# Accumulating DMAs for the residual rows of paired tiles, and a new order of loads in the second value block

## The chip, the cores and the metric

The kernel runs on one core of one Trainium2 chip. The metric is the device time of one execution in microseconds (us). Engine names as in the profile: PE is TensorE, DVE is VectorE, ACT is ScalarE, POOL is GpSimd, SP is the engine that only issues DMAs.

## The reference, cut to what matters

One layer of an encoder trunk on x of shape (2048, 1024), float32: a normalised input is projected to q, k, v and a gate, a 2-D neighbourhood attention mixes the tokens, the gated result is projected back, x is added, and a final normalisation follows.

```python
h = rmsnorm(x, g)
o, gate = neighbourhood_mixer(h, w_in, rpb)
x = x + (o * jax.nn.silu(gate)) @ w_out
return rmsnorm(x, norm_f)
```

The change touches two places: the projection to v (`h @ w_in`, columns of v), and the last line but one, where the residual x is added to the output projection.

## The kernel before, in words

All products are float32 done as three matmuls of split operands: a tile t is split into a high part (ACT copies it, rounding) and a low part (DVE subtracts the high part from t). A 128x512 result in PSUM takes 12 or 24 such matmuls.

The program is one long Python list of instructions. Every engine takes its own instructions in the order in which the Python wrote them, and each one waits for the tiles that it reads and for the buffers that it writes. Tiles come from pools with a fixed number of buffers in rotation (`raw` 6, `kp` 2, `ep` 2, `ev` 8, `rbp` 3, `qp` 2, `xp` 8, `wp` 8); a load into a pool waits until the tile that had the buffer has been read for the last time. SP issues nearly all DMAs, in order, so a load that waits for a buffer holds up every DMA behind it. Some steps are put off: `store(key, lag, f)` (L328) puts `f` into a list that `due(1)`, called after each matmul, works off when `lag` more matmuls have been written.

*Stage two* (`stage_two`, L801) makes q, k, v and the gate for the second half of the tokens. It begins with v: `pair(u, ts, *do)` (L834) writes the matmuls for the 128-token tiles `ts` and the weight block `u` (0 or 1) in four steps, and after step b calls `do[b]`, which holds the side work: `v` evacuates finished tiles, `lw(u, b)` loads two weight tiles into `raw`, `w(u, b)` splits them (L542 on ACT, L545 on DVE), `block`, `t123`, `form` prepare operands for the products that follow. Between them the rows of the output weights are prepared for later: `out_rows(k)` (L886) loads four tiles into `kp` and `ep`, `o(k, "+1")` is a sum on DVE (`out_sum`, L897) and `o(k, "=1")` a split (`out_split`, L904) whose parts SP stores to DRAM. There are four rounds, k = 0 to 3, all in the same four buffers. Then `run()` of `seven_products` starts (L438), whose first operands `ahead(-5)` forms (L420, L421).

*The paired rows.* Tiles 0 to 5 of the output are made singly (`outputs`, L1334). Tiles 6 to 15 go in five pairs, (6,7), (8,9), (10,11), (12,13), (15,14), each with seven products P instead of eight (`rows_product`, L1439), every product 12 matmuls (L1451), in three PSUM banks: P = 1 and 2 in one, 6, 7 and 4 in another, 5 and 3 in the third. A product may write on into its bank only when what must be read in between has been read. For a pair (n0, n1):

- P=1: ACT copies the bank to U1 (L1456). P=2: y of n0, left half (`add_rows`, L1248).
- P=6: DVE writes U6 = bank + U1 (L1461); GpSimd adds the residual x of n0, right half (L1464). P=7: U7 likewise, with x of n1, right half; then GpSimd adds x of n1, left half, to U1 itself (L1468).
- P=5: y of n1, right half = bank + U7. P=4: y of n1, left half = bank + U1, then `finish(n1)`. P=3: y of n0, right half = bank + U6, then `finish(n0)`.

The x tiles come by SP from DRAM (`load_rest_of`, L1434) into `rbp` and `qp`. After each y, ACT squares it and sums the squares (L1251, put off by 5 matmuls). `finish` puts off the root (DVE L1270, ACT L1271, DVE L1272, L1274), the scaling (L1291, two per tile) and the stores (L1295). Tile 14, the last but one, has its y multiplied by the final weights at once (L1256) and its scaling right behind the root (L1287, L1288); tile 15's right half is the last thing evacuated (L1234).

`rows_by_seven` (L1479) writes the order by hand: the first three pairs (E = 3) are interleaved, the last two go one after the other in the order 1, 6, 2, 7, 5, 4, 3. Loads of operands (L1420), their sums (`sum_rows`, L1432), loads of x and the forming of operands (`form_rows`, L1425 on ACT and L1426 on DVE, LEAD products ahead) are written after fixed products of that list.

Of the kernel before, what the change touches and what calls it, by code (L numbers as in the profile page):

```python
# [32 lines left out]
PLAIN = 6  # L33
# [38 lines left out]
def build(ctx, tc, x, xr, xt, wg, rpb, last, w_out, n0, nf, masks, out):  # L72
# [728 lines left out]
    def stage_two():  # L801
# [32 lines left out]
        def pair(u, ts, *do):  # L834
            for b in range(4):
                values_of(X2, u, ts, (2 * b, 2 * b + 1))
                if b < len(do):
                    do[b]()

        def both(*fs):  # L840
            return lambda: [f() for f in fs]
# [10 lines left out]
        def w(u, b):  # L852
            return lambda: [split_v(u, a, b) for a in range(2)]

        def lw(u, *bs):
            return lambda: [load_v0(u, a, b) for b in bs for a in range(2)]

        def v(u, *ts):
            return lambda: [evac_v(u, t, ps[t]) for t in ts]
# [26 lines left out]
        def out_rows(k):  # L886
            def g():
                for q, (r_, c_) in quarters.items():
                    OW[q] = kp([128, 960], F32, "ow")[:, :512] if r_ else ep([128, 512], F32, "ow")
                    nc.sync.dma_start(OW[q], w_out[(4 * r_ + k) * 128:(4 * r_ + k + 1) * 128, c_ * 512:c_ * 512 + 512])  # L890
            return g
# [24 lines left out]
        def o(k, *fs):  # L916
# [4 lines left out]
        pair(0, (10, 11), both(v(0, 8, 9), block("B22", x22, 2, 3)), t123(0), t123(1), both(lw(1, 1), *o(0, "+1")))  # L921
        pair(0, (12, 13), both(v(0, 10, 11), *o(0, "=1", "+3")), both(t123(2), *o(0, "=3", "+2")), both(t123(3), *o(0, "=2", "+4")),
             both(t4(0, 1, 2, 3), lw(1, 2), *o(0, "=4")))
        pair(0, (14, 15), both(v(0, 12, 13), w(1, 0), out_rows(1)), both(w(1, 1), lw(1, 3)), w(1, 2), w(1, 3))
        pair(1, (12,), v(0, 14, 15), both(form("T2", x11, 0), *o(1, "+1")), both(form("T2", x11, 1), *o(1, "=1")), both(*o(1, "+3")))
        pair(1, (13,), both(v(1, 12), form("T2", x11, 2), *o(1, "=3")), both(form("T2", x11, 3), *o(1, "+2")), both(*o(1, "=2", "+4")),
             both(*o(1, "=4")))
        pair(1, (14,), both(v(1, 13), form("T3", x22, 0), out_rows(2)), form("T3", x22, 1), both(), both(*o(2, "+1")))
# [295 lines left out]
    def add_rows(n, j, ps):  # L1224
        xr = RES.pop((n, j))
        state["event"] = clock[0]
        if n not in Y:
            Y[n] = [None, None], tiny.tile([128, 8], F32, name="st3")
        y, st = (raw if j and n < 3 else ev)([128, 512], F32, "y"), Y[n][1]
        Y[n][0][j] = y  # L1230
        if n == tiles - 1:
            cut = [slice(0, 256), slice(256, 512)] if j else [slice(0, 512)]
            for s in cut:
                nc.vector.tensor_tensor(y[:, s], ps[:, s], xr[:, s], OP.add)  # L1234
            for k, s in enumerate(cut):
                to = st[:, (j if k == 0 else 5):(j if k == 0 else 5) + 1]
                nc.scalar.activation(xr[:, s], y[:, s], AF.Square, scale=0.5 ** 0.5, accum_out=to)
            if j == 0:
                nc.vector.tensor_scalar(st[:, 6:7], st[:, 0:1], 0.5 * D * EPS, None, op0=OP.add)
                nc.scalar.activation(st[:, 7:8], st[:, 6:7], AF.Sqrt)  # L1240
            else:
                nc.vector.tensor_scalar(st[:, 7:8], st[:, 1:2], st[:, 6:7], None, op0=OP.add)
            w = ev([128, 512], F32, "yw")
            nc.vector.scalar_tensor_tensor(w, y, 0.5 ** 0.5 / NF_SCALE, late["nf"][j], op0=OP.mult, op1=OP.mult)
            Y[n][0][j] = w
            squared[0] += 1
            return
        nc.vector.tensor_tensor(y, ps, xr, OP.add)  # L1248

        def square():  # L1250
            nc.scalar.activation(xr, y, AF.Square, scale=0.5 ** 0.5, accum_out=st[:, j:j + 1])  # L1251
            squared[0] += 1

        if n == tiles - 2:
            w = ev([128, 512], F32, "yw")
            nc.vector.scalar_tensor_tensor(w, y, 0.5 ** 0.5 / NF_SCALE, late["nf"][j], op0=OP.mult, op1=OP.mult)  # L1256
            Y[n][0][j] = w
        store(("y", n, j), 5, square)

    def finish(n):  # L1260
        y, st = Y[n]
# [172 lines left out]
    def load_rest_of(m, j, k):  # L1434
        n = PAIRS[m][j]
        RES[n, k] = (qp if (j, k) == (1, 0) else rbp)([128, 512], F32, "xr")
        nc.sync.dma_start(RES[n, k], x[n * 128:n * 128 + 128, 512 * k:512 * k + 512])

    def rows_product(m, P):  # L1439
        n0, n1 = PAIRS[m]  # L1440
        if P in (1, 6, 5):
            B[m, P] = bank(512, "py")
            for Q in {1: (2,), 6: (7, 4), 5: (3,)}[P]:
                B[m, Q] = B[m, P]
        t = F.pop((m, P))
        f = uses[P][1]
        for k in range(4):
            c = slice(k * 128, k * 128 + 128)
            xh, xl = TF[f][k]
            for i, (a, b) in enumerate(((0, xh), (0, xl), (1, xh))):  # L1450
                nc.tensor.matmul(B[m, P], t[:, a, c], b, start=P in (1, 6, 5) and k == 0 and i == 0, stop=k == 3 and i == 2,  # L1451
                                 skip_group_check=True)
                due(1)
        if P == 1:
            U[m, 1] = (xp if m == 2 else ep)([128, 512], F32, "p1")
            nc.scalar.activation(U[m, 1], B[m, 1], AF.Copy)  # L1456
        elif P == 2:
            add_rows(n0, 0, B[m, 2])
        elif P in (6, 7):
            U[m, P] = xp([128, 512], F32, "u")  # L1460
            nc.vector.tensor_tensor(U[m, P], B[m, P], U[m, 1], OP.add)  # L1461
            to = (n0, 1) if P == 6 else (n1, 1)
            r = RES.pop(to)
            nc.gpsimd.tensor_tensor(U[m, P], U[m, P], r, OP.add)  # L1464
            RES[to] = U[m, P]
            if P == 7:
                r = RES.pop((n1, 0))
                nc.gpsimd.tensor_tensor(U[m, 1], U[m, 1], r, OP.add)  # L1468
                RES[n1, 0] = U[m, 1]
        elif P == 5:  # L1470
            add_rows(n1, 1, B[m, 5])
        elif P == 4:
            add_rows(n1, 0, B[m, 4])
            finish(n1)
        else:
            add_rows(n0, 1, B[m, 3])
            finish(n0)

    def rows_by_seven():  # L1479
        for f, (r, c) in plain_of.items():  # L1480
            TF[f] = [(woh[4 * r + k, c], wol[4 * r + k, c]) for k in range(4)]
        E, LEAD = 3, 4
        seq = [(m, P) for P in (1, 2) for m in range(E)]
        seq += [(0, 6), (1, 6), (0, 7), (0, 5), (1, 7), (0, 4), (1, 5), (0, 3), (1, 4), (2, 6), (1, 3), (2, 7), (2, 5), (2, 4), (2, 3)]
        seq += [(m, P) for m in range(E, len(PAIRS)) for P in order7]
# [10 lines left out]
            on(i, sum_rows, 2, f)  # L1496
        for i, f in ((2, "A21"), (4, "A22")):
            on(i, load_rows_of, 2, f)
        for i, m, j, k in ((1, 0, 1, 0), (2, 1, 1, 0), (4, 0, 0, 1), (5, 0, 1, 1), (6, 1, 0, 1), (7, 1, 1, 1), (9, 2, 0, 1), (9, 2, 1, 0),
                           (11, 2, 1, 1)):  # L1500
            on(i, load_rest_of, m, j, k)
        for m in range(E, len(PAIRS)):
            s = seq.index((m, 1))
            for d, f in ((-9, "A21"), (-8, "A22"), (-7, "A11"), (-6, "A12")):
                on(s + d, load_rows_of, m, f)
            for d, f in ((-5, "S1"), (-4, "S2"), (-3, "S3"), (-1, "S4")):
                on(s + d, sum_rows, m, f)
            for d, j, k in ((-2, 0, 1), (-2, 0, 0), (-1, 1, 0), (0, 1, 1)):
                on(s + d, load_rest_of, m, j, k)
        for i, s in enumerate(seq):  # L1510
            if i >= 2 * E:
                on(i - LEAD, form_rows, *s)
# [206 lines left out]
```

## Time and profile before

| | us |
|---|---|
| median of 3 runs | 1056.8 |
| the three runs | 1056.8, 1057.53, 1055.7 |
| the profiled execution | 1056.66 |
| its span, first to last instruction | 1054.9 |
| DVE busy in the span | 743.2 |
| ACT busy in the span | 558.4 |
| POOL busy in the span | 278.1 |
| bytes moved | 205.30 MB |

Rows of the timeline are: start in us from the span's start, duration in us, engine, line of the kernel, operation, output and inputs, and in brackets how long the engine had been idle before and what ended that. A row with xN joins N neighbours. "PEld" is the load of a matmul's weights and runs beside PE. "SPq" is an issue on SP's queue, not the transfer. A PE row's end is modelled: a matmul's row is 0.39 us long, while the next one starts sooner.

### The profile page before, as it was taken

To read this page: it belongs to the slowest core of one execution; us is meant where nothing else is said; L and a number is where in the kernel's file an instruction comes from. 1 tells how busy PE (TensorE), PEld (TensorE's weight loads), DVE (VectorE), ACT (ScalarE), POOL (GpSimd) and SP (SyncE) were. 2 spreads that over 40 slices of the span, in tenths; PEclk is the share of its full clock that TensorE was granted. 3 is DMA by queue.
4 is the path that set the end of the run, shared out by engine and by line. 5 is a ranking of instruction groups with operands and counts; after the bars stand their busy time and mean duration, and the time that the engine had idled before them with its cause. 6 is when DMAs were issued, how large, how long until landed. Compare 5 with 4: busy or idle time off the path is not lost.

```text
span 1054.9 us, 20328 instructions
## 1 busy us (share of the span) xinstructions
PE 1039.0 (98%) x7256; PEld 850.1 (81%) x7256; DVE 743.2 (70%) x1601; ACT 558.4 (53%) x1305; POOL 278.1 (26%) x357
## 2 busy tenths in 40 slices
PE   9999999999999989999999999999999999999987
PEld 6888888887888868888888788888888787888776
DVE  5385657778897847655565666667777788777996
ACT  7545323344344435333333477788887877673433
POOL 0000231321221000000000477765565432420331
PEclk9999999999999999999999999999999999999999
DMA  9633444452637568434243787868877689899442
GB/s 312 226 100 100 140 145 129 134 151 96 195 119 211 168 230 293 126 108 132 80 145 121 237 246 218 260 199 279 249 237 247 186 269 312 277 352 354 148 172 80
DMA packets 133213, 205.30 MB, mean 195 GB/s; under 512 B 12216, under 2 KB 56504, under 8 KB 133112
## 3 DMA queue, kind: packets, MB, share of 16 engines
q1 hardware_dynamic: 132680, 203.61, 60.7%
q8 instruction: 57, 0.93, 0.4%
q10 hardware_dynamic: 432, 0.40, 0.1%
q14 instruction: 44, 0.36, 0.1%
HBM read 145.24 MB, written 58.72 MB: 193 GB/s over the span
## 4 chain that ended last, share of the span: by engine, by line
PE 89%; DVE 7%; issue 1%; ACT 1%; DMA 1%; POOL 0%; ACTq 0%; DVEq 0%
PE pp L438 36%; PE pv L562 12%; PE s L1063 8%; PE o L1170 8%; PE py L1451 7%; PE ph L1148 4%; PE pp L384 2%; PE po L1372 2%; PE po L1374 2%; PE pp L386 2%; PE pp L382 2%; PE po L1376 2%; DMA raw<-in_wg_dram 1%; DVE l L521 1%; DVE y L1291 1%
## 5 line engine op out<-in xcount | busy, mean ns | idle before, releaser
L438 PE MATMUL pp<-h,f 128*128 128x512 f32 x672 | 217.6, 389 | 0.0
L1077 ACT ACTIVATE x<-x,st 128x360 f32<-128x360 f32 (+5 forms) x256 | 151.2, 592 | 24.6 <-DVE st L1071 24.6
L438 PEld LDWEIGHTS pp<-h,f 128*128 128x128 f32 x672 | 126.1, 188 | 26.5 <-DVE f L421 0.3
L438 PE MATMUL pp<-t,f 128*128 128x512 f32 x558 | 141.7, 389 | 0.1
L1091 POOL TENSOR_SCALAR x<-x,st 128x480 f32<-128x480 f32 (+5 forms) x192 | 114.4, 613 | 94.1 <-DVE st L1082 91.8
L438 PE MATMUL pp<-l,f 128*128 128x512 f32 x336 | 130.7, 389 | 0.0
L458 POOL TENSOR_TENSOR tmp<-tmp,rb 128x512 f32<-128x512 f32 x36 | 58.4, 1622 | 271.1 <-DVE tmp L456 235.7
L1071 DVE CUSTOM_DVE_ANT_0 x<-s,em 128x360 f32<-128x360 f32 (+5 forms) x256 | 123.0, 535 | 0.3 <-PE s L1063 0.3
L438 PEld LDWEIGHTS pp<-t,f 128*128 128x128 f32 x558 | 104.7, 188 | 22.3 <-DVE u L451 0.6
L1031 POOL TENSOR_TENSOR em<-e,mk 128x264 f32<-128x264 f32 (+3 forms) x64 | 50.8, 825 | 266.2 <-DMA mk<-in_masks_dram 252.7
L421 DVE TENSOR_TENSOR f<-raw,f 128x512 fp32r<-128x512 f32 x105 | 76.5, 728 | 37.4 <-ACT f L420 37.3
L1063 PE MATMUL s<-kt,q 64*128 64x480 f32 (+5 forms) x512 | 95.5, 488 | 0.1
L562 PE MATMUL pv<-wh,h 128*128 128x512 f32 x256 | 90.0, 397 | 4.4 <-ACT wh L542 4.4
L1170 PEld LDWEIGHTS o<-pta,vt 120*64 120x64 f32 (+2 forms) x1792 | 80.9, 137 | 14.4 <-DVE st L1071 13.6
L562 PE MATMUL pv<-wl,h 128*128 128x512 f32 x256 | 89.8, 396 | 0.3 <-DVE wl L545 0.3
L562 PE MATMUL pv<-wh,l 128*128 128x512 f32 x256 | 89.5, 395 | 0.0
L1170 PE MATMUL o<-pta,vt 120*64 120x128 f32 (+5 forms) x1792 | 85.5, 253 | 0.5 <-DVE pta L1124 0.4
L420 ACT ACTIVATE f<-raw 128x512 fp32r<-128x512 f32 x105 | 63.8, 624 | 27.8 <-PE pp L438 12.5
L1063 PEld LDWEIGHTS s<-kt,q 64*128 64x128 f32 x512 | 64.7, 186 | 16.5 <-DVE pta L1124 2.1
L1124 DVE COPY pta<-ph 120x512 f32<-120x512 f32 (+5 forms) x96 | 56.9, 639 | 23.9 <-PE ph L1148 23.8
L438 PEld LDWEIGHTS pp<-l,f 128*128 128x128 f32 x336 | 63.1, 188 | 13.0
L1124 ACT ACTIVATE pta<-ph 120x512 f32<-120x512 f32 (+5 forms) x96 | 49.7, 557 | 37.1 <-PE ph L1148 36.4
(186 smaller groups left out, 1859.6 us busy)
## 6 DMA issues: line engine op xcount, KB each, us to landing
raw<-in_wg_dram SPq DMA_DIRECT2D x124, 256.0 KB, 4.7
row<-in_xr_dram SPq DMA_DIRECT2D x32, 256.0 KB, 4.3
vd<-v SPq DMA_DIRECT2D x32, 256.0 KB, 2.7
sgd<-sg SPq DMA_DIRECT2D x32, 256.0 KB, 2.4
q<-qd SPq DMA_DIRECT2D x32, 256.0 KB, 5.4
sgt<-sgd SPq DMA_DIRECT2D x32, 256.0 KB, 5.6
xr<-in_x_dram SPq DMA_DIRECT2D x32, 256.0 KB, 4.1
ogd<-og SPq DMA_DIRECT2D x32, 256.0 KB, 4.1
```

What stands on the lines that cost most here:

```text
L420: nc.scalar.activation(t[:, 0], src, AF.Copy)
L421: nc.vector.tensor_tensor(t[:, 1], src, t[:, 0].bitcast(F32), OP.subtract)
L438: nc.tensor.matmul(B[n, P], t[:, int(m == 2), c], x[k][int(m == 1)], start=P in (1, 6, 5) and k == 0 and m == 0, stop=k == 3 and m == 2, s ...
L458: nc.gpsimd.tensor_tensor(tmp, tmp, rb[c], OP.mult)
L562: nc.tensor.matmul(ps[t], a[:, o], b, start=k == 0 and m == 0, stop=k == NK - 1 and m == 2)
L1063: nc.tensor.matmul(pst[s], qt[a, qs], kt[a, :r1 - r0, c0:c1].rearrange("p r (s c) -> p s r c", c=8), start=True, stop=True)
L1071: nc.vector.tensor_tensor_reduce(X[i, C][s], pst[s], EM[p, ROW_TYPE[T], COL_TYPE[C], s], -1.0, 1e38, OP.add, OP.min, st[:, o:o + 1])
L1077: nc.scalar.activation(X[i, C][s], X[i, C][s], AF.Exp, bias=st[:, o:o + 1], scale=-1.0, accum_out=st[:, 4 + o:5 + o])
L1091: nc.gpsimd.tensor_scalar(X[i, C][s], X[i, C][s], st[:, o:o + 1], 1.0, op0=OP.mult, op1=OP.mult)
L1124: (nc.vector.tensor_copy if h else lambda o, i_: nc.scalar.activation(o, i_, AF.Copy))(t[:k, h, b * 512:b * 512 + w], banks_[b, h][:k, :w])
L1170: nc.tensor.matmul(to.rearrange("d (h q) -> d h q", q=64) if nq > 64 else to, vt[:k, strip, s * 64:s * 64 + 64], t[:k, h, at:at + 64] if n ...
L1451: nc.tensor.matmul(B[m, P], t[:, a, c], b, start=P in (1, 6, 5) and k == 0 and i == 0, stop=k == 3 and i == 2, skip_group_check=True)
```

## The change

In stage two, `out_rows(1)` moves from step 0 to step 2 of the pair of tiles (14, 15), behind `lw(1, 3)`, and three steps of the same round of output weights move one place later. In the paired rows, `add_rest` issues a DMA from GpSimd's queue that reads x from DRAM and adds it to a tile in SBUF; it replaces the load by SP and the sum on GpSimd for three of the four halves of a pair. For n1's right half it comes after y instead of before, and the square of that half is put off by 14 matmuls instead of 5; tile 14's multiplication moves into the same put-off step. LEAD goes from 4 to 5.

```diff
-        pair(0, (14, 15), both(v(0, 12, 13), w(1, 0), out_rows(1)), both(w(1, 1), lw(1, 3)), w(1, 2), w(1, 3))
-        pair(1, (12,), v(0, 14, 15), both(form("T2", x11, 0), *o(1, "+1")), both(form("T2", x11, 1), *o(1, "=1")), both(*o(1, "+3")))
+        pair(0, (14, 15), both(v(0, 12, 13), w(1, 0)), both(w(1, 1), lw(1, 3)), both(w(1, 2), out_rows(1)), w(1, 3))
+        pair(1, (12,), v(0, 14, 15), form("T2", x11, 0), both(form("T2", x11, 1), *o(1, "+1")), both(*o(1, "=1", "+3")))
...
         def square():
             nc.scalar.activation(xr, y, AF.Square, scale=0.5 ** 0.5, accum_out=st[:, j:j + 1])
             squared[0] += 1
-
-        if n == tiles - 2:
-            w = ev([128, 512], F32, "yw")
-            nc.vector.scalar_tensor_tensor(w, y, 0.5 ** 0.5 / NF_SCALE, late["nf"][j], op0=OP.mult, op1=OP.mult)
-            Y[n][0][j] = w
-        store(("y", n, j), 5, square)
+            if n == tiles - 2:
+                w = Y[n][0][j] = ev([128, 512], F32, "yw")
+                nc.vector.scalar_tensor_tensor(w, y, 0.5 ** 0.5 / NF_SCALE, late["nf"][j], op0=OP.mult, op1=OP.mult)
+
+        after = n >= PLAIN and (n, j) in {(b, 1) for _, b in PAIRS}
+        if after:
+            add_rest(n, j, y)
+        store(("y", n, j), 14 if after else 5, square)
...
+    def add_rest(n, j, to):
+        nc.gpsimd.dma_start(to, x[n * 128:n * 128 + 128, 512 * j:512 * j + 512], accum_op=OP.add)
+
...
             to = (n0, 1) if P == 6 else (n1, 1)
-            r = RES.pop(to)
-            nc.gpsimd.tensor_tensor(U[m, P], U[m, P], r, OP.add)
             RES[to] = U[m, P]
-            if P == 7:
-                r = RES.pop((n1, 0))
-                nc.gpsimd.tensor_tensor(U[m, 1], U[m, 1], r, OP.add)
+            if P == 6:
+                add_rest(n0, 1, U[m, 6])
+            else:
+                add_rest(n1, 0, U[m, 1])
                 RES[n1, 0] = U[m, 1]
...
-        E, LEAD = 3, 4
+        E, LEAD = 3, 5
...
-        for i, m, j, k in ((1, 0, 1, 0), (2, 1, 1, 0), (4, 0, 0, 1), (5, 0, 1, 1), (6, 1, 0, 1), (7, 1, 1, 1), (9, 2, 0, 1), (9, 2, 1, 0),
-                           (11, 2, 1, 1)):
-            on(i, load_rest_of, m, j, k)
...
-            for d, j, k in ((-2, 0, 1), (-2, 0, 0), (-1, 1, 0), (0, 1, 1)):
-                on(s + d, load_rest_of, m, j, k)
+            on(s - 2, load_rest_of, m, 0, 0)
```

## The prediction

> **What bounds the kernel now.** I read the page first, then the waits of TensorE, then the two places where it waits.
>
> ```profile
> PE 1039.0 (98%) x7256; PEld 850.1 (81%) x7256; DVE 743.2 (70%) x1601; ACT 558.4 (53%) x1305; POOL 278.1 (26%) x357
> ```
>
> TensorE is busy 98% of the span. So this change, which removes no matmul, can win only what TensorE loses to waiting and to a reduced clock, and the tail after the last matmul. The waits of TensorE, longest first (total, times, longest):
>
> ```profile
> PE pv L562 <- ACT wh L542: 4.4, 2, 3.7
> PE py L1451 <- DVE y L1248: 2.2, 1, 2.2
> ```
>
> The first lies in the diff's first hunk (value products, second weight block), the second in the paired rows. The timeline of TensorE around the first:
>
> ```profile
> 373.88 0.39 PE L562 MATMUL pv<-wh,l 128*128 128x512 f32 x1
> 377.95 0.51 PE L562 MATMUL pv<-wh,h 128*128 128x512 f32 x1 [3.67 <-ACT wh L542]
> ...
> 382.74 0.39 PE L562 MATMUL pv<-wh,l 128*128 128x512 f32 x1
> ```
>
> and a one-microsecond window after it (PE, PEld, DVE, ACT, POOL, then granted clock, DMA share, GB/s):
>
> ```profile
> 380.00:381.00 1.00, 1.00 (x4) 0.81 (x3) 1.00 (x3) 0.20 (x1) 0.00 (x0) 0.50 1.02 304
> ```
>
> After the wait the granted clock is 0.50 for a while. The matmul at 382.74 is the twelfth after 373.88. Undisturbed matmuls come 0.227 us apart, by this row of the paired rows' stage (the end of the last one is 0.39 after its start, so (5.83-0.39)/24):
>
> ```profile
> 1037.84 5.83 PE L1451 MATMUL py<-t,f 128*128 128x512 f32 x25
> ```
>
> Twelve take 2.7 us; they took 8.9. **The first place loses 6.1 us.** The second: the paired rows are 35 products of 12 matmuls, the first starts here,
>
> ```profile
> 949.61 0.50 PE L1451 MATMUL py<-woh,f 128*128 128x512 f32 x1
> ```
>
> and the 32nd (P=7 of the last pair) at 1037.84. 31 x 12 x 0.227 = 84.3 us; it took 88.2. **The second place loses 3.9 us.** Ten us is the most that is to be had.
>
> **The first hunk: queue order.** The queue of SP, in order:
>
> ```profile
> 362.83 0.93 SPq L533 DMA_DIRECT2D raw<-in_wg_dram  x2
> ...
> 366.45 1.94 SPq L890 DMA_DIRECT2D ow<-in_w_out_dram  x4
> 368.49 0.93 SPq L397 DMA_DIRECT2D vd<-v  x2
> 369.61 1.37 SPq L533 DMA_DIRECT2D raw<-in_wg_dram  x2
> ```
>
> ScalarE's conversions of these weights (start, duration, idle before and what ended it):
>
> ```profile
> 367.31 1.17 ACT L542 ACTIVATE wh<-raw 128x512 fp32r<-128x512 f32 x2 [0.51 <-DMA raw<-in_wg_dram]
> 376.75 1.15 ACT L542 ACTIVATE wh<-raw 128x512 fp32r<-128x512 f32 x2 [8.27 <-DMA raw<-in_wg_dram]
> ```
>
> The last weights of the second value block are issued at 369.61 behind four output-weight loads and two stores, and usable 7.1 us later; the pair issued at 362.83 into a nearly empty queue took 4.5. After the change the stores come first at 366.45, then these loads at about 367.4, then the output weights. With 4.5 to 7.1 us they are usable at 371.9 to 374.5. TensorE wants them about 374.1, so most of its wait goes in either case. I take 5.3, nearer the lower end because two stores still stand ahead but the four loads don't: 372.7.
>
> What is late next? VectorE's chain of output-weight sums (L897) and splits, in its own order:
>
> ```profile
> 380.03 0.68 DVE L897 TENSOR_TENSOR ow<-ow 128x512 f32<-128x512 f32 x1
> ...
> 394.26 0.69 DVE L897 TENSOR_TENSOR ow<-ow 128x512 f32<-128x512 f32 x1 [3.82 <-DMA ow<-in_w_out_dram]
> ...
> 419.39 0.69 DVE L421 TENSOR_TENSOR f<-raw,f 128x512 fp32r<-128x512 f32 x1 [0.31 <-ACT f L420]
> ```
>
> ```profile
> 419.68 0.39 PE L438 MATMUL pp<-h,f 128*128 128x512 f32 x1
> ```
>
> Between 380.03 and 419.39 it is not TensorE that paces it: each round of output weights loads into the buffers of the round before (the wait at 394.26). At its end stands the first operand of the products that begin at 419.68, only just ready. The chain starts 3.3 us after the conversion (376.75 to 380.03); the change puts one more 0.6 us split ahead of its first sum, so 3.9: 376.6, that is 3.4 us sooner. TensorE could be there 6.1 us sooner and will wait for the chain, some 2.7 us. **I take -3.4 us** (-1.6 if the loads still need 7.1, -6.1 if the chain should have slack).
>
> **The paired rows: GpSimd's sums go.** Fifteen sums (three in each of five pairs) leave GpSimd and fifteen loads leave SP. What they did to VectorE, GpSimd first:
>
> ```profile
> 1002.53 1.62 POOL L1464 TENSOR_TENSOR u<-u,xr 128x512 f32<-128x512 f32 x1 [4.49 <-ACT f L1425]
> 1004.11 1.73 POOL L1468 TENSOR_TENSOR p<-p,xr 128x512 f32<-128x512 f32 x1
> ```
>
> ```profile
> 1002.91 1.79 DVE L1426 TENSOR_TENSOR f<-raw,f 128x512 fp32r<-128x512 f32 x1
> 1004.62 2.43 DVE L1291 SCALAR_TENSOR_TENSOR y<-y,st,acc 128x512 f32<-128x512 f32 x2
> ...
> 1012.21 0.69 DVE L1426 TENSOR_TENSOR f<-raw,f 128x512 fp32r<-128x512 f32 x1
> 1012.82 1.41 DVE L1291 SCALAR_TENSOR_TENSOR y<-y,st,acc 128x512 f32<-128x512 f32 x2
> ```
>
> The same two operations take 1.1 and 1.0 us longer beside GpSimd. That is 2.1 us of lateness just ahead of the 2.2 us for which TensorE waits on VectorE's y. [...] Without the sums I count the second place's **-3.9 us** as won; the floor of this gain is 0, the ceiling all of it. One step more of LEAD moves each form one product earlier, in work that VectorE does anyway: nothing.
>
> **What the accumulating DMAs add** is a wait. Call X the time from a row tile being ready to the landing of its accumulated x. The trace has no accumulating DMA and none from GpSimd. The nearest rows are the loads they replace, those of the paired rows (from issue, min/median/max) and those of all x tiles (median):
>
> ```profile
> DMA to landing us min/median/max: 2.8/3.0/5.5
> ```
>
> ```profile
> xr<-in_x_dram SPq DMA_DIRECT2D x32, 256.0 KB, 4.1
> ```
>
> Below, X can't be less than 2.8, as it moves the same bytes. Above I set 5.5 + 1.6 = 7.1: the slowest such load plus a GpSimd operation's time for making the descriptors and the read of the destination. I take 4.1, the row in the middle, about one microsecond over a quiet load.
>
> GpSimd has nothing else to do here, so the issues wait only for their data, and the fifteen loads that leave SP had nobody of TensorE's behind them. Two of the three DMAs of a pair have time: U6's is used five products later, U1's two (5.4 us). The third, on y of the second row's right half, has a square of ScalarE waiting (now 14 matmuls, 3.2 us, behind the product instead of 5). ScalarE's next forms stand behind that square, but have a lead of five products; the price lies elsewhere: behind the squares stands VectorE's root (L1270), behind which stand the evacuations that TensorE waits for. Pair four in VectorE's order:
>
> ```profile
> 1024.63 0.68 DVE L1248 TENSOR_TENSOR y<-py,u 128x512 f32<-128x512 f32 x1
> ...
> 1028.70 0.21 DVE L1270 TENSOR_SCALAR st<-st 128x1 f32<-128x1 f32 x1 [0.19 <-ACT p L1251]
> ...
> 1029.88 0.69 DVE L1248 TENSOR_TENSOR y<-py,u 128x512 f32<-128x512 f32 x1 [0.34 <-PE py L1451]
> ...
> 1036.43 0.68 DVE L1461 TENSOR_TENSOR u<-py,p 128x512 f32<-128x512 f32 x1
> ```
>
> ```profile
> 1046.98 0.64 ACT L1251 ACTIVATE p<-y 128x512 f32<-128x512 f32 x1 [1.99 <-DVE y L1248]
> ```
>
> y is ready at 1025.3. Then X, then two squares; one costs 0.75 (from 1046.98 to the root at 1047.73, quoted below). The root starts at 1025.35 + X + 1.5 = 1026.85 + X, and the evacuation of 1029.88 follows 0.84 after it (1.18 less the idle 0.34): 1027.7 + X, at X = 4.1 1.9 us late. The work up to u (1036.43 to 1037.1) shifts with it, and the product of 1037.84 must not start before u has left the bank: 0.7 of slack. TensorE waits X - 2.9 = 1.2 us. Pairs three and four have this; the first two, interleaved, have three products more between. **+2.4 us** (0 to 8.4).
>
> **The tail**, on the last pair:
>
> ```profile
> 1043.53 0.69 DVE L1248 TENSOR_TENSOR y<-py,u 128x512 f32<-128x512 f32 x1 [1.73 <-POOL u L1464]
> ...
> 1047.73 0.21 DVE L1270 TENSOR_SCALAR st<-st 128x1 f32<-128x1 f32 x1
> ...
> 1048.92 0.76 DVE L1234 TENSOR_TENSOR y<-py,u 128x256 f32<-128x256 f32 x2
> ```
>
> The last evacuation (1048.92) stands behind the root and scaling of the tile before, which take 1.2 from 1047.73. That root will need 1044.2 + X + 1.5; the evacuation starts at 1046.9 + X, X - 2.0 late. Tile 14's two scaled copies (L1256) move behind the landing too; VectorE does them beside ScalarE's two squares, which take longer. **+2.1 us** (0.8 to 5.1).
>
> **Sum**: -3.4 - 3.9 + 2.4 + 2.1 = -2.8. The profiled execution took 1056.66 (span 1054.9 and 1.8 around it), beside a median of 1056.8: **1053.9 us**.
>
> [...]
>
> **Rivals.**
> How busy the engines and the DMA queues are near the end (columns as above, ten microseconds):
>
> ```profile
> 1030.00:1040.00 10.00, 10.00 (x46) 8.28 (x45) 7.88 (x16) 3.42 (x10) 1.67 (x1) 1.00 0.28 107
> ```
>
> *Landing like a plain quiet load*, X = 2.8. For it: the DMA engines are 28% busy there. [...] -3.4 - 3.9 + 0 + 0.8 = -6.5: 1050.2. Chance 0.22.
> *Slow accumulation (the slower side).* [...] From X = 5.7 it decides: 2(X-2.9) + X - 2.0 exceeds the 7.3 won by 2.1. At X = 7.1: +8.4 + 5.1 - 7.3 = +6.2, 1062.9. [...] Against: 5.5 is the slowest load seen here. Chance 0.20. [...]
> *The weights come no sooner*: the second block's loads need raw buffers that VectorE still has to split:
>
> ```profile
> 365.96 3.69 DVE L545 TENSOR_TENSOR wl<-raw,wh 128x512 fp32r<-128x512 f32 x6
> ```
>
> If they wait for all six splits, to 369.7, they are issued no earlier than before; the first term is 0: 1057.3. Against: two buffers are enough, and the first two splits end at 367.2. Chance 0.10.
>
> **How the numbers follow.** The forecast gets 0.48. About 0.2% (2.1 us) can be told from no change; X up to 4.3 keeps the forecast beyond it, and I give a fifth of its chance to X between 4.3 and 5.7, which is no change. Faster: 0.38 + 0.22 = 0.60. Same: 0.10 + 0.10 = 0.20. Slower: 0.20. Cases of both signs hold chance; the forecast's own range is 1050.5 to 1057. The whole range is 1048.5 (quiet landing and 1.7 more from the weights) to 1060.5 (X about 6.3).
>
> **What would show it.** Right: no wait of pv on wh near 374, a wait of 2 to 3 us of the next products on a split f near 414; VectorE's L1426 and L1291 at 0.69 and 1.41 throughout; a root L1270 held 2 us by a square; the last evacuation 2 us after TensorE's end. Wrong: a GpSimd issue that lasts several us, ScalarE idle at squares for more than X = 5.7, or a wait on weights that stays.

## The result: 1063.7 us, slower, and the profile after

| | before | after |
|---|---|---|
| median of five runs each, us | 1056.8 (1055.7 to 1057.53) | 1063.73 (1060.57 to 1064.78) |
| ratio to before, 95% interval | | 1.0062 (1.0044 to 1.0079) |
| profiled execution / its span, us | 1056.66 / 1054.9 | 1063.73 / 1062.0 |

The forecast was 1053.9 (1048.5 to 1060.5). The kernel became 0.6% slower, outside the range and on the other side.

The line numbers move a little: root L1272 to L1276, square still L1251, scaling L1293, forms L1427 (ScalarE) and L1428 (VectorE), product L1456, copy of P=1 L1461, U6 and U7 L1466, the accumulating DMA L1442, tile 14's multiplication L1255.

First the busy times of the page after, as the prediction showed them of before:

```profile
PE 1040.7 (98%) x7256; PEld 850.0 (80%) x7256; DVE 734.9 (69%) x1601; ACT 558.5 (53%) x1305; POOL 267.6 (25%) x357
```

VectorE has 8 us less to do and TensorE is as busy as before; shares of busy time show nothing of the 6.9 us. The waits view of TensorE does (engine, line, what it waited for; total, times, longest):

```profile
PE py L1456 <- ACT p L1461: 4.1, 2, 3.4
PE py L1456 <- ACT f L1427: 2.4, 2, 1.8
PE pv L562 <- ACT wh L542: 2.2, 1, 2.2
PE pp L438 <- ACT f L420: 1.8, 1, 1.8
```

The wait on the value weights shrank (3.7 before). One wait of 2.2 on y is gone from the paired rows, and four others have come, on copies and forms of ScalarE. The waits view of ScalarE from 930 on names what it waited for itself:

```profile
ACT u L1251 <- DMA y<-in_x_dram: 24.4, 5, 8.5
```

Five squares, one per pair, wait for the DMA that adds x onto y. (Not all 24.4 us are lost: ScalarE would have idled for part of it.) The timeline of pair three shows how that reaches TensorE. Rows of four engines after, in order of time:

```profile
1005.15 0.69 DVE L1248 TENSOR_TENSOR y<-py,u 128x512 f32<-128x512 f32 x1
1006.20 0.87 POOL L1442 DMA_DIRECT2D y<-in_x_dram  x1 [3.11 <-DVE y L1248]
1011.85 0.63 ACT L1251 ACTIVATE u<-y 128x512 f32<-128x512 f32 x1 [4.60 <-DMA y<-in_x_dram]
1013.22 0.21 DVE L1272 TENSOR_SCALAR st<-st 128x1 f32<-128x1 f32 x1 [4.97 <-ACT p L1251]
1014.00 0.69 DVE L1248 TENSOR_TENSOR y<-py,u 128x512 f32<-128x512 f32 x1
1017.38 0.20 ACT L1273 ACTIVATE st<-st 128x1 f32<-128x1 f32 x1 [1.93 <-DVE st L1272]
1017.49 0.58 ACT L1461 ACTIVATE p<-py 128x512 f32<-128x512 f32 x1
1018.12 0.80 PE L1456 MATMUL py<-woh,f 128*128 128x512 f32 x1 [3.38 <-ACT p L1461]
```

y is ready at 1005.84, its x has landed at 1011.85: X is 6.0 us. The square waits, VectorE's root (L1272) stands idle 4.97 us behind it, the next evacuation (1014.00) behind the root. ScalarE makes its squares, the roots (the last one, 1017.38, waits for VectorE once more) and at last the copy of the next pair's P=1 (1017.49). TensorE, which has the next product's operand (P=2) but not the bank, waits 3.38. And it pays again when it resumes. One-microsecond windows (PE, PEld, DVE, ACT, POOL, then granted clock, DMA share, GB/s):

```profile
1017.00:1018.00 1.00, 0.00 (x0) 0.00 (x0) 0.67 (x4) 0.62 (x3) 0.00 (x0) 0.83 0.59 231
1018.00:1019.00 1.00, 0.88 (x2) 0.78 (x3) 0.38 (x1) 1.00 (x3) 0.00 (x0) 0.50 0.77 293
1020.00:1021.00 1.00, 1.00 (x4) 0.81 (x3) 1.00 (x2) 0.00 (x0) 0.00 (x0) 0.50 0.15 59
```

The granted clock is 0.50, and matmuls start 0.43 us apart instead of 0.227. It fell in the last third of a microsecond before 1018, while TensorE still waited. A drop of the clock comes also after the waits of 1.84 at 415 (0.50 from 416.9 to 420.3) and of 1.83 in the paired rows (0.50 from 997.2 to 1000.6). The second of these is the work of pair two; ScalarE, VectorE and TensorE:

```profile
990.27 0.63 ACT L1251 ACTIVATE u<-y 128x512 f32<-128x512 f32 x1 [4.49 <-DMA y<-in_x_dram]
991.64 0.21 DVE L1272 TENSOR_SCALAR st<-st 128x1 f32<-128x1 f32 x1 [2.18 <-ACT u L1251]
995.71 0.68 DVE L1466 TENSOR_TENSOR u<-py,p 128x512 f32<-128x512 f32 x1
996.54 7.54 PE L1456 MATMUL py<-t,f 128*128 128x512 f32 x25 [1.83 <-ACT f L1427]
```

The view names a form of ScalarE that ended at 996.45. But that form is for a later product; this one (P=7 of pair three) writes on into the bank of U6, whose evacuation ended at 996.39, so I take U6 as what it waited for. Its twenty-five matmuls take 7.54 us; the row of the prediction had 5.83. The tail, VectorE after:

```profile
1053.47 1.29 DVE L1255 SCALAR_TENSOR_TENSOR yw<-y,acc 128x512 f32<-128x512 f32 x2 [1.58 <-DMA y<-in_x_dram]
1054.90 0.21 DVE L1272 TENSOR_SCALAR st<-st 128x1 f32<-128x1 f32 x1
...
1055.98 0.75 DVE L1234 TENSOR_TENSOR y<-py,u 128x256 f32<-128x256 f32 x2
```

TensorE's last matmul starts at 1053.50 and the last evacuation only 2.48 later (0.43 before).

Where the 7.1 us of span come from, by four stretches of the two timelines:

| stretch | before | after | difference |
|---|---|---|---|
| start to the last value matmul ahead of the wait on weights | 373.88 | 370.92 | -2.96 |
| from there to the first product on t (L438) | 48.66 | 49.26 | +0.60 |
| first product of the paired rows to TensorE's last matmul | 98.88 | 106.19 | +7.31 |
| that matmul to the last evacuation | 0.43 | 2.48 | +2.05 |

The rest (the products in between, the last scaling and store) differs by 0.1. The first row is no part of the change: the program there is the same, and over 17 profiles of before, after and the experiments this matmul starts at 373.9 (before), 373.1 (one with the old stage two) and 370.9 to 372.0 (the other fifteen, one with the old stage two among them). The difference is made in the first 11 us. TensorE's first twelve value matmuls and the one behind them, before and then after:

```profile
5.54 1.22 PE L562 MATMUL pv<-wh,h 128*128 128x512 f32 x2 [0.76 <-ACT wh L542]
...
10.74 1.08 PE L562 MATMUL pv<-wh,h 128*128 128x512 f32 x4
```

```profile
4.47 0.73 PE L562 MATMUL pv<-wh,h 128*128 128x512 f32 x2
...
7.78 1.08 PE L562 MATMUL pv<-wh,h 128*128 128x512 f32 x4
```

Before, the twelve start 1.1 us later and take 5.2 us instead of 3.3: they come 0.43 us apart, although the granted clock reads 1.00 over these 12 us in both profiles; the cause is not shown. So one execution can be 3 us off by when TensorE gets its first weights and by the pace of its first matmuls. The ratios from many runs, not the one profile, carry the small differences below.

### The profile page after: what moved, and what is told of

Read it like the earlier page. It is cut to its first block, busy times and chain, and to the rows that moved or that the text cites. A ratio compares the mean times of both kernels' runs of the same rounds, so it can differ in the third digit from the quotient of the medians.

```text
span 1062.0 us, 20328 instructions
## 1 busy us (share of the span) xinstructions
PE 1040.7 (98%) x7256; PEld 850.0 (80%) x7256; DVE 734.9 (69%) x1601; ACT 558.5 (53%) x1305; POOL 267.6 (25%) x357
## 5 line engine op out<-in xcount | busy, mean ns | idle before, releaser
L438 PE MATMUL pp<-h,f 128*128 128x512 f32 x672 | 218.8, 391 | 1.8 <-ACT f L420 1.8
L438 PEld LDWEIGHTS pp<-h,f 128*128 128x128 f32 x672 | 126.7, 189 | 29.1 <-ACT f L420 2.3
L438 PE MATMUL pp<-t,f 128*128 128x512 f32 x558 | 141.8, 389 | 0.1
L438 PE MATMUL pp<-l,f 128*128 128x512 f32 x336 | 131.4, 391 | 0.0
L438 PEld LDWEIGHTS pp<-t,f 128*128 128x128 f32 x558 | 104.9, 188 | 22.4 <-DVE u L451 0.6
L438 PEld LDWEIGHTS pp<-l,f 128*128 128x128 f32 x336 | 63.4, 189 | 13.1
```

Source lines behind the costliest of these rows:

```text
L438: nc.tensor.matmul(B[n, P], t[:, int(m == 2), c], x[k][int(m == 1)], start=P in (1, 6, 5) and k == 0 and m == 0, stop=k == 3 and m == 2, s ...
```

## The experiments

The theory: the loss is **one wait**, that of the square and the root of each pair's second row on the DMA that adds x onto y, passed on through ScalarE's and VectorE's order; and TensorE's waits cost more than their length. The rivals: the fifteen DMAs cost wherever they stand (GpSimd's time for their issue, traffic); the first hunk costs or wins several us.

All medians are device times; each group of kernels ran beside its own runs of before (medians 1055.4, 1055.8, 1055.9, 1056.1). "Paired rows" is the start of the first product to the start of the last matmul in the profile; 35 products of 12 matmuls at 0.227 would be 95.1.

| kernel | median us | ratio to before, 95% | paired rows | tail |
|---|---|---|---|---|
| before (first profile) | 1056.8 | | 98.9 | 0.4 |
| after (first profile) | 1063.7 | 1.0062 (1.0044 to 1.0079) | 106.2 | 2.5 |
| stage two alone | 1054.1 | 0.9984 (0.9967 to 1.0001) | 99.9 | 0.4 |
| paired rows alone | 1064.9 | 1.0084 (1.0057 to 1.0112) | 107.7 | 2.7 |
| right half by sums | 1050.3 | 0.9945 (0.9928 to 0.9962) | 96.6 | 0.8 |
| last pair by sums | 1061.1 | 1.0050 (1.0032 to 1.0069) | 110.2 | 0.6 |
| plain copy, one run | 1056.8 | | 101.1 | 1.5 |
| roots later | 1057.7 | 1.0020 (1.0009 to 1.0032) | 101.7 | 2.7 |
| more DMAs | 1054.0 | 0.9985 (0.9970 to 1.0000) | 98.9 | 0.7 |
| sums, old stage two | 1053.1 | 0.9976 (0.9964 to 0.9987) | 97.4 | 0.6 |
| sums again | 1050.7 | 0.9956 (0.9944 to 0.9969) | 96.4 | 0.8 |
| sums, LEAD 4 | 1050.5 | 0.9953 (0.9941 to 0.9966) | 96.6 | 1.1 |
| roots last | 1053.6 | 0.9980 (0.9969 to 0.9992) | 98.9 | 2.6 |
| more adds | 1055.9 | 0.9993 (0.9981 to 1.0004) | 103.8 | 0.8 |
| after again | 1062.5 | 1.0057 (1.0039 to 1.0075) | 107.0 | 2.4 |
| traffic at the tail | 1065.4 | 1.0096 (1.0072 to 1.0120) | 105.6 | 5.5 |
| filled waits | 1063.2 | 1.0066 (1.0048 to 1.0083) | 105.3 | 2.6 |

**The two hunks apart.** Before with the first hunk of the change only, and after with that hunk undone.

> The kernel before with the first hunk alone (order of loads and output-weight rounds in stage two). The prediction: -3.4, so about 1053.4. Theory now, from the trace after: TensorE's wait on the second block's weights is shortened by 3.2 us, but 1.8 us of wait and some 1.9 us at granted clock 0.50 come back at the products near 415, so the start of those products moves by less than 1 us beside the last value matmul before the wait: 1056 to 1058, no difference that can be measured. Rival: the 3 us by which the profiled execution after is early at 50 us belong to this hunk, not to chance: then about 1054. The last value matmul before the wait stands at 373.9 if the early start is not in this kernel, at 371 if it is.

> The kernel after with the first hunk undone: the accumulating DMAs, the later square and LEAD 5 alone. The prediction: -3.9 + 2.4 + 2.1 = +0.6, so 1057.4. Theory now, from the trace after (paired rows +7.3, tail +2.1): 1064 to 1066, with waits of ScalarE's squares on the accumulating DMA of over 4 us, and TensorE's waits on the copy p and on the forms behind u as after. Rival: the loss hangs on the new order of stage two as well (what its stores and loads leave behind in the queues): then under 1062.

The hunks add up: 0.9984 and 1.0084 against 1.0062 together. All of the loss is in the paired rows; stage two wins 1.7 us (3.5 to nothing), more than I then expected and less than the 3.4 of the prediction. Its median of 1054.1 and its last value matmul at 371.0 are what the rival named, but before took 1055.4 beside it, and the early start is not the hunk's (above). Stage two alone, the weights and the wait at the end of the chain:

```profile
372.23 0.50 PE L562 MATMUL pv<-wh,h 128*128 128x512 f32 x1 [0.85 <-ACT wh L542]
...
414.02 0.50 PE L438 MATMUL pp<-h,f 128*128 128x512 f32 x1 [1.55 <-ACT f L420]
...
417.16 2.88 PE L438 MATMUL pp<-t,f 128*128 128x512 f32 x12
```

From the last value matmul (370.99) to 417.16 are 46.17 us, 2.5 less than before, while in the kernel after it was 49.26: there the wait at 415 was 1.84 and the clock fell behind it, here 1.55 and it did not. Over the fourteen profiles with the new order this stretch took 46.2 to 47.8 us in the eight without a drop of the clock at these products, and 48.3 to 49.3 in the six with one; the three with the old order took 48.4 to 49.3. So in one execution the hunk wins 1 to 3 us here or nothing, by what the clock does.

**The second row's right half as before, the other two DMAs kept.**

```diff
-        after = n >= PLAIN and (n, j) in {(b, 1) for _, b in PAIRS}
+        after = False
...
+                r = RES.pop((n1, 1))
+                nc.gpsimd.tensor_tensor(U[m, 7], U[m, 7], r, OP.add)
...
+            on(s, load_rest_of, m, 1, 1)
```

> The kernel after, but the residual of the second row's right half comes as before (load by SP, sum on GpSimd onto U7 ahead of y, square put off by 5 matmuls); the other two halves of each pair keep their accumulating DMAs. Theory (the loss is the wait of the squares and roots on that one DMA): TensorE's waits on the copy p and the tail's 2.1 us go, one stretched operation of VectorE per pair comes back; 9.4 less some 2 for the stretching: 1054 to 1058. Rival (the accumulating DMAs cost wherever they stand, by GpSimd's descriptor work or by the traffic): two thirds of the loss stays, 1060 to 1062.

It is faster than both kernels, and better than the theory's numbers. TensorE's waits view of it, all waits from 0.5 us up:

```profile
PE pp L438 <- ACT f L420: 1.6, 1, 1.6
PE zp L126 <- DVE z L123: 1.2, 1, 1.2
PE pv L562 <- ACT wh L542: 1.1, 1, 1.1
PE py L1456 <- DVE y L1248: 0.6, 1, 0.6
```

Of the waits of the paired rows one of 0.6 us is left. One DMA out of three per pair carried the whole loss: 11 to 12 us between this kernel and the one after. The ten accumulating DMAs that it keeps (on U6 and U1) hold up nobody.

**The last pair only.**

```diff
-        after = n >= PLAIN and (n, j) in {(b, 1) for _, b in PAIRS}
+        after = n >= PLAIN and (n, j) in {(b, 1) for _, b in PAIRS[:-1]}
```

(and its x loaded and summed as in the kernel above)

> The kernel after, with the second row's right half of the last pair alone done as before (load and GpSimd sum, square put off by 5). Theory: only the tail's 2.1 us come back, less the old wait of 1.7 us for GpSimd's sum ahead of y, which stood in the tail before too: 1061.6. Rival: the last evacuation stands behind something else than the root of tile 14, and nothing is won: 1063.7.

The tail falls from 2.5 to 0.6, and the ratio from 1.0062 to 1.0050, with overlapping intervals: the size fits, the time can't prove it. Its profile shows another 4 us in the paired rows, where nothing differs up to the last pair: two drops of the clock after a wait of 4.72 and one after 1.90. Like waits, of 2.25 and 2.28, drew none in one execution and one in another (below).

**Accumulation or queue?**

```diff
-            add_rest(n, j, y)
+            nc.gpsimd.dma_start(y, x[n * 128:n * 128 + 128, 512 * j:512 * j + 512])
```

> The kernel after, with the DMA on y of the second row's right half a plain copy from the same GpSimd queue instead of an accumulation: x replaces that half of y, which is no longer the reference's. It moves the same bytes into SBUF but needn't read the destination. Theory A (X, 4.5 to 5.9 us from y to its landing, is the price of the accumulation): the copy lands 2.8 to 3.0 us after its issue, like the loads on SP's queue, the squares wait about 1.5 us less in pairs three and four, and the time falls to some 1057. Theory B (X is the price of GpSimd's queue and descriptors): landing stays at 3.8 to 5.6 us and the time at 1061 to 1065.

Theory A holds in kind; its sizes hold in the tail alone. GpSimd's issue and the wait behind it in the tail, first this kernel, then the one after:

```profile
1043.67 0.57 POOL L1259 DMA_DIRECT2D y<-in_x_dram  x1 [1.79 <-DVE y L1248]
1046.55 0.63 ACT L1251 ACTIVATE u<-y 128x512 f32<-128x512 f32 x1 [7.53 <-DMA y<-in_x_dram]
```

```profile
1049.68 0.86 POOL L1442 DMA_DIRECT2D y<-in_x_dram  x1 [1.77 <-DVE y L1248]
1053.53 0.63 ACT L1251 ACTIVATE u<-y 128x512 f32<-128x512 f32 x1 [8.54 <-DMA y<-in_x_dram]
```

Issue to use is 2.88 for the copy and 3.85 for the accumulation: 0.3 more in the issue and 0.7 more afterwards. There the copy from GpSimd's queue is as quick as the loads on SP's that I had taken as a bound (2.8 to 3.0). In the first four pairs the copy took 3.3, 3.3, 5.3 and 3.3 us, the accumulation 4.7, 4.2, 5.7 and 4.2: the accumulation is 0.4 to 1.4 us longer, and in pair three the copy was slow as well. The squares of pairs three and four waited 0.4 and 1.0 us less, not 1.5. The time of one run proves little: its waits of 2.15 at 416 and 3.35 in the paired rows drew no drop of the clock, where after's had drawn one each time.

**The DMAs kept, the roots put off.** Two kernels; the second one's edit:

```diff
-        store(("y", n, j), 14 if after else 5, square)
+        store(("y", n, j), (14 if n == tiles - 2 else 40) if after else 5, square)
...
-            store(("y", n), 12, root)
+            store(("y", n), 32 if n in (7, 9, 11, 13) else 12, root)
```

(scaling 38, stores 50; the first kernel had 30, 30 and 36)

> The kernel after, all DMAs kept, but for the first four pairs the square of the second row's right half is put off by 30 matmuls instead of 14, the root behind it by 30 instead of 12 and its scaling by 36 instead of 24, so that neither ScalarE nor VectorE reaches them before the accumulated x has landed. Theory (the loss is waiting in the order of the two engines, not the DMAs): the waits of TensorE on the copy p and on the forms behind u go, and the time is the kernel's with the right half by sums plus the tail's 2 us, 1051 to 1054. Rival (the DMAs' own traffic): 1060 or more. Second rival: ScalarE's forms now stand behind the later squares and TensorE waits for them: 1056 to 1060.

> The kernel after, all fifteen accumulating DMAs kept, with the square of the second row's right half put off by 40 matmuls (9.1 us), its root by 32, scaling 38 and stores 50 behind the left half, for the first four pairs. With 30 and 30 the square of pair three still waited 2.5 us, because its DMA took 6.7 us to land, and ScalarE's square root of the other row and VectorE's reciprocal stood behind it. Now nobody should wait except in the tail. Theory (the loss in the pairs is waiting in order): the paired rows take 97 to 98.5 us from the first product to the last matmul (106.2 after, 101.7 with 30 and 30, 96.6 with the right half by sums), the tail is 2 us late: 1052 to 1055. Rival (contention on the DMA engines delays operands and stores as well): waits of ScalarE's or VectorE's forms on loads of operands take their place, 1056 or more.

The first missed its range: 1057.7. That lies in the second rival's range, but TensorE's longest wait in its paired rows, 2.35, is on VectorE's U6 and not on a form. ScalarE and VectorE of it in pair three:

```profile
1011.49 0.63 ACT L1251 ACTIVATE u<-y 128x512 f32<-128x512 f32 x1 [2.49 <-DMA y<-in_x_dram]
```

```profile
1009.36 0.21 DVE L1272 TENSOR_SCALAR st<-st 128x1 f32<-128x1 f32 x1
1012.34 0.16 DVE L1274 RECIPROCAL st<-st 128x1 f32<-128x1 f32 x1 [2.77 <-ACT st L1273]
```

Thirty matmuls weren't enough: its DMA had been issued at 1004.75 and took 6.7 us, and now the other row's square root (L1273) stood behind the waiting square. With 40 the kernel takes 1053.6, in the middle of what the theory gave (its paired rows, 98.9, are 0.4 over) and 0.2% under before. So 8 to 10 of the 11 to 12 us go although all fifteen DMAs are still there, by changing only the order in which two engines come to the data. What is left over the kernel with sums is the tail's 1.8 and, in this profile, 2.3 in the paired rows, where the square of pair three still waits 1.25: issued at 1003.87, used at 1011.80.

**More DMAs for nobody.** On the kernel with sums, a spare accumulating DMA after each P=6 and P=7; the second time without the extra loads:

```diff
+            add_rest(0, 0, d)
```

> The kernel with the right half by sums, plus ten accumulating DMAs (two per pair) onto a spare tile that nobody waits for, and ten loads of that tile: the number of accumulating DMAs is doubled. Theory (they cost only where somebody waits): no difference from the kernel with the right half by sums beside it (its ratio to before was 0.9945): 1050 to 1052. Rival (each costs by GpSimd's descriptor work or traffic): the ten would cost as much as the ten that are there, 2 us or more: 1053 and above.

> The kernel with the right half by sums and ten more accumulating DMAs onto two spare tiles that nobody waits for, but only two more loads instead of ten. The kernel with ten such DMAs and ten loads had 1.1 us of wait on a form and its paired rows took 2.3 us longer. If the accumulating DMAs alone do this (they hold the DMA engines, in which operands' loads stand), the same 1.5 to 2.5 us more than the base; if the extra loads did it, within 0.5 us of the base.

Both are slower by 4 to 5 us than the kernel with sums: the first as its rival says, the second (5.2 over its base) by more than either of its theories. But it is a wait again. GpSimd and VectorE of the second one in pair one:

```profile
976.95 0.86 POOL L1442 DMA_DIRECT2D xr<-in_x_dram  x1 [4.96 <-DMA xr<-in_x_dram]
977.51 1.61 POOL L1475 TENSOR_TENSOR u<-u,xr 128x512 f32<-128x512 f32 x1
979.16 0.69 DVE L1248 TENSOR_TENSOR y<-py,u 128x512 f32<-128x512 f32 x1 [7.05 <-POOL u L1475]
```

In pairs one and two the spare DMA adds onto a tile on which an earlier DMA is still under way, so its issue waits (up to 4.2 us in the first kernel, 4.96 here), and the sum on U7 that y needs stands behind it on GpSimd. VectorE waits 7.05 us for that sum, and TensorE later 4.75, with two drops of the clock (1.14 and 0.87 and no drop in the first kernel). My experiment had built the fault that it was to exclude. Where no issue waited (six spare DMAs in pairs three to five) TensorE has no wait more than 0.3 us longer than without them. What the DMAs cost by traffic alone these two kernels don't tell.

**Why pair three is slow, and what the clock does.** Three kernels on one chip: after again; after with three loads beside the tail's DMA; after with matmuls for nobody in two of TensorE's waits.

```diff
+        if (n, j) == (tiles - 2, 1):
+            for pl in (qp, qp, rbp):
+                d = pl([128, 512], F32, 'xr')
+                nc.vector.memset(d[:, 0:1], 0.0)
+                nc.sync.dma_start(d, x[0:128, 0:512])
```

```diff
+        fill_ = {(2, 7): 6, (3, 2): 12}.get((m, P), 0)
+        if fill_:
+            zb = bank(512, 'zb')
+            for _ in range(fill_):
+                nc.tensor.matmul(zb, t[:, 0, 0:128], TF[f][0][0], start=True, stop=True)
```

> The kernel after once more, as the base of this group and for a second profile: 1061 to 1065, ratio 1.005 to 1.008. In its profile the same waits as in the first one; where a wait of about 2 us is followed by granted clock 0.50 may differ, since in twelve kernels waits of 1.8 to 2.4 us were followed by it 8 times in 12.

> The kernel after, with three more loads of 256 KB on SP's queue onto spare tiles, issued just when the last pair's y of the right half is ready, so that they are in flight with the accumulating DMA on it, as the three loads of operands are in pair three. Theory (pair three's long landing is shared DMA engines): from GpSimd's issue to the square the tail takes 5.5 to 6 us instead of 3.85 (1049.68 to 1053.53 after), and the kernel is about 2 us slower than the kernel after beside it. Rival (pair three is slow for another reason, such as VectorE's work at that time): it stays at 3.8 to 4.2, and the time is the same.

> The kernel after, with 6 matmuls onto a bank that nobody reads ahead of the product P=7 of pair three (idle 1.83 us after) and 12 ahead of P=2 of pair four (idle 3.38 us after): 1.4 and 2.7 us of TensorE's work, all in time that it spent waiting. Theory (idleness sets off the 3.4 us at clock 0.50): the two drops go, each is worth 1.7 us, and the kernel is 2 to 3.4 us faster than the kernel after beside it. Rival (the drops come with the load on the chip at that place and not from the wait): they stay, and the time is the same or up to 1 us longer.

The kernel after again was as slow as the first time; its wait of 1.56 at the first place drew no drop, the one of 4.59 at the second drew two. In pair three after, SP issues operands of the next pair just as GpSimd issues its DMA at 1006.20:

```profile
1005.70 2.89 SPq L1422 DMA_DIRECT2D raw<-ogd  x3
```

With three such loads in the tail, SP, GpSimd and ScalarE there:

```profile
1047.88 1.34 SPq L1261 DMA_DIRECT2D xr<-in_x_dram  x3
```

```profile
1048.33 0.86 POOL L1447 DMA_DIRECT2D y<-in_x_dram  x1 [1.76 <-DVE xr L1260]
1055.23 0.63 ACT L1251 ACTIVATE u<-y 128x512 f32<-128x512 f32 x1 [11.54 <-DMA y<-in_x_dram]
```

6.9 us instead of 3.85, and the tail 5.5 instead of 2.4; 1065.4 beside 1062.5, so 3 to 4 us. Shown: three loads on SP's queue lengthened this landing by 3 us in the tail; that the three loads of operands do it in pair three is inferred.

The filled waits: both drops of the clock are gone from the paired rows, and TensorE in pair three and at the next pair reads

```profile
993.36 1.52 PE L1456 MATMUL zb<-t,f 128*128 128x512 f32 x6
995.38 5.96 PE L1461 MATMUL py<-t,f 128*128 128x512 f32 x25 [0.50 <-DVE u L1471]
...
1012.82 2.88 PE L1456 MATMUL zb<-woh,f 128*128 128x512 f32 x12
1017.53 0.50 PE L1461 MATMUL py<-woh,f 128*128 128x512 f32 x1 [1.83 <-ACT p L1466]
```

25 matmuls take 5.96 instead of 7.54. But the time is 1063.2 beside 1062.5: no gain. The trace shows 105.3 for the paired rows (the 18 spare matmuls, 4.1 us, included) against 106.2 and 107.0. TensorE came 1.1 us sooner to the next y (its DMA is issued 57.8 us after the first product instead of 58.9), but that DMA then took 6.5 us instead of 5.65: it landed with the loads beside it, 64.3 and 64.5 us after the first product. The won time was waited away behind the landing. The drops went with the idleness, in one profile; and in all 17 no drop in stage two or the paired rows came without a wait of at least 1.35 us, in which it began or which it followed within 1.7 us. So in these profiles the drops go with the waits, and not with the place alone. That they cost 3 us of device time in this kernel is not shown.

**Two smaller questions**, on the kernel with sums: stage two as before, and LEAD 4.

```diff
-        E, LEAD = 3, 5
+        E, LEAD = 3, 4
```

> The kernel with the right half by sums, and stage two as before (first hunk undone). Paired rows: like the kernel with the right half by sums, which lost only 1.5 us there against 3.8 before. Stage two: the hunk was worth 2.3 to 2.5 us from the last value matmul ahead of the wait to the products (46.2 to 46.8 us in three kernels, 48.7 and 49.3 without it). So about 2.5 us more than that kernel: 1052.8. If the three profiles with the hunk that were 2 us early at 50 us were so by chance, the last value matmul ahead of the wait can stand anywhere from 371 to 374; if the hunk makes it early, it stands at 373 to 374 here and the time is nearer 1055.

> The kernel with the right half by sums and LEAD 4 as before. My prediction put the step of LEAD at nothing: the same time as with LEAD 5. Rival: with LEAD 5 VectorE makes forms ahead of evacuations, so LEAD 4 is some 1 us faster, or ScalarE's wait for sums needs the longer lead and LEAD 4 is 1 to 2 us slower.

> The kernel with the right half by sums once more, as the base of this group and to see how far a second set of runs and a second profile agree: 1050 to 1052, ratio 0.993 to 0.997. In its profile the waits ahead of the paired rows' products should again stay under 1 us, so no product of theirs should run at granted clock 0.50.

The old stage two gives 1053.1, as expected to 0.3; with the hunk the kernel with sums is 2 to 3 us faster (0.9945 to 0.9956 against 0.9976, in other groups of runs). LEAD makes no difference: 1050.5 and 1050.7.

The last of the three expectations held: 1050.7, waits of at most 0.6 in the paired rows and no drop there. **The best version** is therefore the change with the second row's right half left to GpSimd's sum, 0.9945 to 0.9956 of before, with LEAD 4 or 5.

## Why the prediction was wrong, point by point

- **The first hunk, -3.4.** Right in kind, too large: 1.7 to 3 by the times, the lower end not clear of nothing. The weights were usable 6.3 us after their issue in stage two alone (364.63 to 370.91) and 6.5 and 8.2 after it in the kernel after, against my 5.3. The chain of output-weight sums decided, as I said, and TensorE's wait for it was 1.4 to 2.6 in twelve of the fourteen profiles with the new order (2.7 predicted). Not costed: the clock behind that wait, which took the gain back in six of them.
- **GpSimd's sums go, -3.9.** The stretched operations are gone (0.68 and 1.41 throughout), and in the kernel with sums, which still has one GpSimd sum per pair, the paired rows lose 1.3 to 1.5 us instead of 3.8. Right, some 2.4 of it.
- **The landing, X = 4.1.** From y ready to the square it was 5.0, 4.5, 6.0, 4.6 and 4.4 in the five pairs: inside my bounds of 2.8 to 7.1, but over the value I chose. (The 1.6 for GpSimd in the upper bound was my estimate; no run shows it, and the fifteen issues lasted 0.86 to 1.02.) Two things lay outside my nearest rows: the accumulation is longer than a plain copy (by 1.0 us in the tail, 0.4 to 1.4 in the pairs), and my DMA share of 28% came from 1030 to 1040, not from pair three. There the trace of before, just behind this y (1006.98 to 1007.66), has the DMA engines 91% busy (last column but one):

```profile
1008.00:1009.00 1.00, 1.00 (x5) 0.81 (x5) 1.00 (x3) 0.93 (x3) 0.00 (x0) 1.00 0.91 303
```

- **The wait that takes the place of the old one, +2.4: the step that failed.** The chain began as I described (DMA, square, root, evacuation), but three things in the step were wrong. First, "pairs three and four have this; the first two, interleaved, have three products more between": pair two waited as well, its root 2.18 us behind the same square, and TensorE 1.83 for U6 of pair three behind that root. Second, I counted a wait of TensorE as its length: in after's paired rows two waits drew a drop of the clock, which cost 1.7 and 1.5 us (the second began 0.5 us before TensorE resumed). Third, I followed VectorE's order alone, to U6 and P=7 of the next pair. Behind pairs three and four TensorE waited one product sooner, at P=2, for ScalarE's copy of the bank of P=1, which stands behind the other row's square root. So it is luck that X - 2.9 gives 3.1 for pair three, where 3.38 was measured; for pair four it gives 1.7, measured 0.67. Together 1.83 + 3.38 + 0.67 + 3.2 (clock) = 9.1, of the 9.6 between this kernel's paired rows and those with sums. Of the 6.7 by which the term was too small, the clock is 3.2, pair two 1.8 and pair three 2.2, less 0.5 in pair four.
- **The tail, +2.1.** Right: 2.05, with X = 4.4 instead of 4.1.
- **The rivals.** "Slow accumulation" was the case that came, at 0.20: its condition (X from 5.7 on, my sign for it too) was met in pair three alone, and its time of 1062.9 is 0.8 from the result, partly by the terms that I had left out. The GpSimd issue of several us that I named as a sign of being wrong did not show: none of the fifteen lasted over 1.02 us. "Weights no sooner" did not happen: they were issued at 364.56.

Summed with the sizes measured: -2 (stage two), -2.4 (sums), +9.1 (waits and clock), +2.1 (tail) is +6.8; measured 6.9. The first size is from medians and the others from single profiles, so the close fit is in part luck.

## What to carry to other kernels

Before handing a sum to a DMA, ask who reads the result next and what stands behind that reader on its engine: two DMAs of each pair whose result is read products later held up nobody, the third, read by a square of ScalarE soon after, cost 11 us. Take the transfer's duration from the very place where it will run, with the loads in flight there (3.85 us in the tail here, 6.9 there beside three loads), not from a median or a neighbouring quiet stretch. If such a DMA must stay, put the reader and all that depends on it behind it in the order by more than the slowest landing (here 30 matmuls were too few, and 40 still left a wait of 1.25 us).

## What the runs showed of the hardware

*The granted clock and TensorE's waits.* In 17 profiles every drop in stage two and the paired rows lasted 3.4 us at granted clock 0.50, or twice that. Half of it was lost where TensorE worked throughout (the 25 matmuls of 7.54 us instead of 5.83), less where the drop began within the wait (1.5 us behind the 3.38 in the kernel after). Waits of TensorE from 1.2 to 1.75 us drew one in 2 cases of 15, from 1.83 to 2.56 in 10 of 15, from 3.08 to 3.72 in 5 of 6 (once two), and from 4.5 on two in 4 of 4. Waits of 2.25 and 2.28 at the same place went either way; before, and stage two alone (its eight matmuls from 1001.68 took 3.4 us instead of 1.8):

```profile
1007.80 0.47 PE L1451 MATMUL py<-woh,f 128*128 128x512 f32 x1 [2.25 <-DVE y L1248]
...
1008.34 0.62 PE L1451 MATMUL py<-woh,f 128*128 128x512 f32 x2
```

```profile
1001.13 0.47 PE L1451 MATMUL py<-woh,f 128*128 128x512 f32 x1 [2.28 <-DVE y L1248]
...
1001.68 1.05 PE L1451 MATMUL py<-woh,f 128*128 128x512 f32 x2
```

*An accumulating DMA from GpSimd*, 256 KB: issue 0.86 to 1.02 us in the kernel after (0.57 for a plain copy), use 3.7 to 4.1 us after the start of the issue in the tail (2.9 for the copy), 5.6 to 6.9 beside three loads of the same size, once 7.9.
